# A mixer layer with product-key experts: scatters and first-stage gathers kept in the program's order on GpSimd, and a list's sort cut into four parts with a dense block between

## The chip, the cores and the metric

One core of a Trainium2 chip runs the whole kernel. The metric is the device time of one execution in microseconds; lower is better.

## The reference

One layer on 512 tokens of width 2048. A mixer (attention with forget gates beside a gated linear recurrence) comes first; its part of the kernel is not touched. Then comes the expert layer (PEER), where the change is:

```python
s1 = einsum(q[..., 0, :], k1); s2 = einsum(q[..., 1, :], k2)
v1, i1 = top_k(s1, 16); v2, i2 = top_k(s2, 16)
vs, ic = top_k(v1[..., :, None] + v2[..., None, :], 16)
e = i1[ic // 16] * 128 + i2[ic % 16]
w = softmax(vs)
act = gelu(einsum('thkd,td->thk', u[e], h)) * w
y = einsum('thk,thkd->td', act, vt[e])
```

Every token has 8 heads and picks 16 of 16384 experts in each. `u` and `vt` hold one row of 2048 floats for each expert. All arithmetic is in fp32; a matrix product is made of three products of a rounded and a remainder part.

## The kernel before

**Four token tiles of 128.** Three of them go through a dense first stage: for each of 128 blocks of 128 experts, `ublock` (L680) multiplies the block of `u` with the three tiles, applies gelu and stores the result in two tables in DRAM (`tab2`, `tab1`). The fourth tile is done row by row beside it, the *side work* (`side_work`, L748): 128 gathers of `u` rows, each followed by a product with the tokens on VectorE (L757), then 128 gathers of `v` rows, each added to a sum (L755). One gather brings one row for each of 128 tokens, 1 MB.

**A dense block** is two halves. Each half loads 512 KB of `u` on SyncE's queue (L98), rounds it on ScalarE (L93), takes the remainder on VectorE (L94), does 24 matmuls (L689) and ends with a call of `pump()`. A pump runs two things: 0.9 of a side gather (the gather on GpSimd, and the VectorE step for the gather two before), and one scatter, if any is queued. So 128 blocks carry 256 pumps and some 231 of the 258 side steps; the rest is sent out in the second stage, in equal shares over the first 68 chunks.

**Two lists** tell the second stage which experts any token of a tile uses. Making one has four steps.
- `halves_of` (L899): the weights of a tile are spread with one-hot products into `ws` (L906 to L913), 64 tokens at a time; each half ends with four stores of 1 MB into a table (L917) and four maxima (L918). Between the groups of four tokens it calls `ublocks`, at a pace set by `BH` or `BL`.
- `make_list` (L833): each of the 128 partitions sorts its 128 block numbers in descending order. A round is `V.max` (the eight largest, L821) and `V.match_replace` (strikes them out, L822); 16 rounds sort all. List 0, for two tiles, first sorts two short own lists of three rounds each.
- 16 or 20 columns that overflow are scattered by row to a list in DRAM: one indirect DMA on GpSimd for each column (L883, `one(i)`), queued in `scatters`, and at the end the read-back on SyncE's queue (L887).
- Between list 0 and list 1 the tokens of the third dense tile go through `topk` (L931 loads, L587 to L603) and `decode`.

**The second stage** goes through 171 chunks of 128 experts. `vchunk` gathers 128 `v` rows (1 MB) and their gelu values (`raw`), multiplies, splits and accumulates in PSUM (L988).

**What sets the order.** The source is traced from top to bottom; that is the program's order. When the program is built, each engine's and queue's instructions are put in one fixed order by simulating it: whenever an engine is free it gets, among the instructions whose inputs and buffers are ready by then, the one that stands first in the program. So what is ready early runs ahead of what is traced before it. `tc.keep_in_program_order(ins)` adds an order edge from the instruction that was traced just before `ins` on the same engine: `ins` is put behind it in that engine's order. It adds no semaphore wait. On the chip each engine follows its fixed order.

The calls of `ublocks` before: blocks 0 to 2 at the start, to 71 by the end of list 0's halves, then list 0's sort, to 75, `topk` to 81, list 1's halves to 116, list 1's sort, and to 128.

Of the kernel before, what the change touches and what calls it, by code (L numbers as in the profile page):

```python
# [27 lines left out]
LISTS = ((48, 16, 4), (66, 20, 5))  # L28
NONE = 24
B0 = 3  # L30
BH = 18
BL = 20
GRATE = 0.9
GLAG = 2
NAR = 5
# [23 lines left out]
def program(ctx: ExitStack, tc: tile.TileContext, a):  # L59
    nc = tc.nc  # L60
    V, A, PE, G = nc.vector, nc.scalar, nc.tensor, nc.gpsimd
# [45 lines left out]
    def rstd(pool, ss, n, scale):  # L107
        v = pool.tile([128, 16], F32, name="rs", tag="rs", bufs=4)[:, :n]
        A.activation(v, ss, AF.Sqrt, bias=eps, scale=scale)
        V.reciprocal(v, v)  # L110
        return v
# [23 lines left out]
    for half in range(2):  # L135
        r = raw.tile([128, 1024], F32, name="raw")[:1]
# [28 lines left out]
    def bank():  # L165
        return ps.tile([128, 512], F32, name="ps", tag="ps")
# [13 lines left out]
    with tc.tile_pool(name="pro", bufs=1, reuse_waits="tile") as pro:  # L180
# [7 lines left out]
        for t in range(NT):  # L188
# [7 lines left out]
            r = rstd(pro, ss, 1, 1.0 / D)  # L196
# [362 lines left out]
    with tc.tile_pool(name="wk2", bufs=12, reuse_waits="tile") as wk2:  # L559
        for q in range(4):  # L560
            pr = bank()
            for k4 in range(4):
                k = q * 4 + k4
# [81 lines left out]
    for h in range(H):  # L645
# [6 lines left out]
        for half in range(2):  # L652
            p = pbank()
            for hv in range(2):
                wh, wl = stream(a["w_q"][h * 2 + half, hv])
                for k8 in range(8):
                    k = hv * 8 + k8
# [7 lines left out]
            c0 = half * 128  # L665
# [16 lines left out]
    def ublock(b):  # L682
        p = pbank()
        for half in range(2):
            uh, ul = stream(a["peer_u"][b, half])
            for k8 in range(8):
                k = half * 8 + k8
                for i, (l, r) in enumerate(three(uh, ul, dh[k], dl[k])):
                    PE.matmul(p[:, :NDT], l[:, k8 * 128:k8 * 128 + 128], r, start=(k == 0 and i == 0),  # L689
                              stop=(k == KC - 1 and i == 2))  # L690
            pump()
        ge = gq.tile([128, NDT], F32, name="ge")
        A.activation(ge, p[:, :NDT], AF.Gelu_apprx_tanh)  # L693
        rows = slice(128 + b * 128, 256 + b * 128)
        nc.sync.dma_start(tab2[rows].rearrange("p (t x) -> p t x", t=2)[:, :, 0:128],
                          ge[:, 128:384].rearrange("p (t x) -> p t x", t=2))
        nc.sync.dma_start(tab1[rows, 0:128], ge[:, 0:128])
# [5 lines left out]
    blk = [0]  # L703
# [6 lines left out]
    def ublocks(upto):  # L710
        while blk[0] < upto:
            ublock(blk[0])
            blk[0] += 1
# [9 lines left out]
    ei = late.tile([128, H * 16], I32, name="ei")  # L723
# [16 lines left out]
    tabs = (tab2, tab1)  # L740

    def gather(out, src, idx):
        G.indirect_dma_start(out=out, out_offset=None, in_=src,  # L743
                             in_offset=bass.IndirectOffsetOnAxis(ap=idx, axis=0))

    NSIDE = 2 * H * 16 + GLAG

    def side_work():  # L748
        held = []
        n = H * 16  # L750

        def use():
            v, j, r = held.pop(0)
            if v:
                V.scalar_tensor_tensor(out=y0, in0=r, scalar=dots[:, j:j + 1], in1=y0, op0=OP.mult, op1=OP.add)  # L755
                return
            V.scalar_tensor_tensor(out=r, in0=r, scalar=1.0, in1=hrow, op0=OP.mult, op1=OP.mult,  # L757
                                   accum_out=dots[:, j:j + 1])
            if j == n - 1:
                A.activation(dots, dots, AF.Gelu_apprx_tanh)  # L760
                V.tensor_tensor(out=dots, in0=dots, in1=ew, op=OP.mult)

        for v in range(2):
            for j in range(n):
                r = gb.tile([128, D], F32, name="gr")
                gather(r, a["v_rows" if v else "u_rows"], ei[:, j:j + 1])
                held.append((v, j, r))
                if len(held) > GLAG:
                    use()
                yield  # L770
        while held:
            use()
            yield

    class Side:
        def __init__(self):
            self.it = side_work()
            self.n = 0
            self.due = 0.0
# [38 lines left out]
    def rounds(L, vals, n):  # L818
        for k in range(n):
            sl = slice(k * 8, k * 8 + 8)  # L820
            V.max(L[:, sl], vals[k % 2])  # L821
            V.match_replace(vals[1 - k % 2], L[:, sl], vals[k % 2], 0.0)  # L822
        return vals[n % 2]

    def rows_of(L, n, nm):
# [6 lines left out]
    def make_list(lt, Fs, n):  # L832
        c0, r, _ = LISTS[n]  # L833
        own = []
        cnt = lt.tile([128, 2], F32, name="lcnt")
        vals = [lt.tile([128, 128], F32, name=f"lv{i}") for i in range(2)]
        L = lt.tile([128, 128], F32, name="lf")
        fs = [lt.tile([128, 128], F32, name=f"lu{i}") for i in range(len(Fs))]
        for f, F in zip(fs, Fs):
            V.scalar_tensor_tensor(out=f, in0=F, scalar=0.0, in1=iota1, op0=OP.is_gt, op1=OP.mult)  # L840
        if len(Fs) == 1:
            V.tensor_copy(vals[0], fs[0])
        else:
            both = lt.tile([128, 128], F32, name="lboth")
            V.tensor_tensor(out=both, in0=fs[0], in1=fs[1], op=OP.min)
            for f in fs:
                V.tensor_tensor(out=f, in0=f, in1=both, op=OP.subtract)
            for i, f in enumerate(fs):
                rest = rounds(L, [f, vals[0]], NONE // 8)
                ig, iv = rows_of(L, NONE, f"own{i}")  # L850
                V.tensor_scalar(ig, ig, 2, i, op0=OP.mult, op1=OP.add)
                own.append((ig, iv))
                V.tensor_tensor(out=both, in0=both, in1=rest, op=OP.add)
            V.tensor_copy(vals[0], both)
        V.tensor_scalar(L, vals[0], 0.0, None, op0=OP.is_gt)
        V.tensor_reduce(cnt[:, 0:1], L, axis=AX.X, op=OP.add)
        rounds(L, vals, 16)
        ig, iv = rows_of(L, 128, n)
        V.tensor_scalar(cnt[:, 1:2], cnt[:, 0:1], float(-c0 - r), 0.0, op0=OP.add, op1=OP.max)
        V.tensor_scalar(cnt[:, 0:1], cnt[:, 0:1], float(-c0), 0.0, op0=OP.add, op1=OP.max)  # L860
        V.tensor_scalar(cnt[:, 0:1], cnt[:, 0:1], float(r), None, op0=OP.min)
        p = bank()
        PE.matmul(p[:, 0:1], tri, cnt[:, 0:1], start=True, stop=True)
        PE.matmul(p[:, 1:3], ones, cnt, start=True, stop=True)
        tot = lp1.tile([128, 3], F32, name=f"off{n}")
        V.tensor_copy(tot, p[:, 0:3])
        pos = lt.tile([128, 32], U32, name="lpos")[:, :r]
        V.tensor_scalar(pos, iota[:, :r], tot[:, 0:1], None, op0=OP.add)
        pc = lt.tile([128, 2, 32], U32, name="lpc")[:, :, :r]
        V.tensor_scalar(pc[:, 0], pos, 127, None, op0=OP.bitwise_and)  # L870
        V.tensor_scalar(pc[:, 1], pos, 7, None, op0=OP.logical_shift_right)
        pf = lt.tile([128, 2, 32], F32, name="lpf")[:, :, :r]
        V.tensor_copy(pf, pc)
        V.scalar_tensor_tensor(out=pf[:, 0], in0=pf[:, 0], scalar=float(r), in1=pf[:, 1], op0=OP.mult, op1=OP.add)
        V.tensor_scalar(pf[:, 1], iota[:, :r], cnt[:, 0:1], 65536.0, op0=OP.is_ge, op1=OP.mult)
        idx = lp1.tile([128, 32], I32, name=f"lidx{n}")[:, :r]
        V.tensor_tensor(out=idx, in0=pf[:, 0], in1=pf[:, 1], op=OP.add)
        views = dram_disjoint_views(lists[n], r)
        sg = lp1.tile([128, r], I32, name=f"sg{n}")
        sv = lp1.tile([128, r], I32, name=f"sv{n}")  # L880

        def one(i):
            G.indirect_dma_start(out=views[i], out_offset=bass.IndirectOffsetOnAxis(ap=idx[:, i:i + 1], axis=0),  # L883
                                 in_=ig[:, c0 + i:c0 + i + 1], in_offset=None, bounds_check=128 * r - 1, oob_is_err=False)

        def done():
            nc.sync.dma_start(sg, lists[n].rearrange("(p c) o -> p (c o)", p=128))  # L887
            V.tensor_scalar(sv, sg, -128, 0, op0=OP.add, op1=OP.max)

        scatters.extend([lambda i=i: one(i) for i in range(r)] + [done])  # L890
        return (ig, iv), (sg, sv), tot, own

# [30 lines left out]
    with tc.tile_pool(name="dz", bufs=1, reuse_waits="tile") as dz:  # L923
        Fs = [halves_of(dz, t, oT[t], tab2, t * 256 + 128, B0 + 2 * t * BH, BH) for t in range(2)]
        sets[0] = make_list(dz, Fs, 0)
    ublocks(B0 + 4 * BH)
    with tc.tile_pool(name="tp0", bufs=1, reuse_waits="tile") as tp0:
        tt0 = topk_tiles(tp0, 1)
        for h in range(H):
# [3 lines left out]
            if h % 2:  # L933
                ublocks(B0 + 4 * BH + h // 2 + 1)
        rows(decode(tp0, tt0))
        ublocks(B0 + 4 * BH + 6)
    with tc.tile_pool(name="dz2", bufs=1, reuse_waits="tile") as dz:
        sets[1] = make_list(dz, [halves_of(dz, 0, oT[2], tab1, 128, B0 + 4 * BH + 6, BL)], 1)
        ublocks(NB)
# [173 lines left out]
    r = inv(1)  # L1113
# [75 lines left out]
```

## Time and profile before

| | |
|---|---|
| median of 3 runs | 3143.48 us (3142.44 to 3146.86) |
| the profiled execution | 3144.75 us, of which the span is 3142.9 us |
| PE busy | 2872.5 us (91%) |
| VectorE (DVE) busy | 2487.0 us (79%) |
| ScalarE (ACT) busy | 1220.9 us (39%) |
| GpSimd (POOL) busy | 944.1 us (30%) |
| DMA | 869.31 MB, mean 277 GB/s |

All terms below are reckoned on the profiled execution; it is 1.27 us above the median. The dense stage lies between 1075 and 2380 us of the span, the second stage behind it. PEclk (the granted clock) is a share of TensorE's 2.4 GHz, DMA the mean busy share of 16 DMA engines.

### The profile page before, as it was taken

Reading aid. Unit: us, or ns where it says so; the run is one execution under the profiler, and the core shown is the slowest. Engines: PE = TensorE matmul, PEld = TensorE weight load, DVE = VectorE, ACT = ScalarE, POOL = GpSimd, SP = SyncE. Lnnn points to the kernel's source line nnn. Section 1 sums busy time; section 2 is a strip of 40 time slices with the busy share of each in tenths; the row PEclk is TensorE's granted clock in tenths of the full one; section 3 lists DMA queues with packets and bytes.
Section 4 is the critical chain, followed back from the end, with each engine's and each line's share of the span. In section 5 each row is a group of like instructions: output and inputs, shape, how many; then the busy total and the mean of one; then the engine's idle time right before and its main releaser. Section 6 shows DMA issues by size and latency. Waiting matters only on the chain.

```text
span 3142.9 us, 39160 instructions
## 1 busy us (share of the span) xinstructions
PE 2872.5 (91%) x14093; PEld 2501.5 (80%) x14093; DVE 2487.0 (79%) x4100; ACT 1220.9 (39%) x1653; POOL 944.1 (30%) x673
## 2 busy tenths in 40 slices
PE   7899999989999999988878999889998899988887
PEld 5677777778788899988868999879996688766665
DVE  6877777763368899999989998968888866677787
ACT  5322223662232333433322343413223455556665
POOL 0000000000020033222242322264447645567774
PEclk9999899999999999999988999989999999999998
DMA  9867777333322389999989999989999977779896
GB/s 343 291 222 235 239 236 238 106 107 128 114 90 94 117 297 379 340 306 295 294 270 357 351 347 352 314 319 404 404 403 386 386 278 272 260 270 344 320 327 228
DMA packets 329503, 869.31 MB, mean 277 GB/s; under 512 B 125682, under 2 KB 181362, under 8 KB 274388
## 3 DMA queue, kind: packets, MB, share of 16 engines
q0 software_dynamic: 72512, 477.03, 40.4%
q1 hardware_dynamic: 256352, 389.52, 36.8%
q8 instruction: 112, 1.84, 0.2%
q14 instruction: 91, 0.75, 0.1%
q10 hardware_dynamic: 436, 0.18, 0.0%
HBM read 805.38 MB, written 61.25 MB: 276 GB/s over the span
## 4 chain that ended last, share of the span: by engine, by line
PE 53%; DVE 17%; DMA 15%; issue 8%; ACT 3%; POOL 2%; SPq 1%; DVEq 0%; POOLq 0%; ACTq 0%
PE pj L689 25%; DMA araw<-w_ada 8%; PE ps L988 7%; PE pj L659 6%; DVE slo L94 5%; PE ps L525 4%; DVE gr L757 3%; PE pj L301 2%; PE ps L219 2%; DMA raw<-tab,ig 2%; DVE araw L147 2%; PE ps L912 2%; PE pj L988 1%; PE pj L525 1%; DMA tab<-ws 1%
## 5 line engine op out<-in xcount | busy, mean ns | idle before, releaser
L689 PE MATMUL pj<-dh,slo 128*128 128x384 f32 x2048 | 698.3, 343 | 59.4 <-DVE slo L94 57.9
L689 PE MATMUL pj<-dh,shi 128*128 128x384 f32 x2048 | 699.1, 341 | 29.0 <-ACT shi L93 26.4
L689 PE MATMUL pj<-dl,shi 128*128 128x384 f32 x2048 | 694.8, 339 | 1.3 <-issue 1.3
L93 ACT CAST shi<-raw 128x1024 fp32r<-128x1024 f32 (+1 forms) x402 | 418.3, 1048 | 634.1 <-PE pj L689 219.0
L94 DVE TENSOR_TENSOR slo<-raw,shi 128x1024 fp32r<-128x1024 f32 (+1 forms) x402 | 485.1, 1214 | 214.3 <-ACT shi L93 200.1
L689 PEld LDWEIGHTS pj<-dh,slo 128*128 128x128 f32 x2048 | 392.1, 192 | 70.6 <-DVE slo L94 68.7
L94 DVE TENSOR_TENSOR slo<-gr,shi 128x1024 fp32r<-128x1024 f32 x342 | 407.2, 1220 | 39.6 <-ACT shi L93 38.1
L689 PEld LDWEIGHTS pj<-dh,shi 128*128 128x128 f32 x2048 | 393.0, 192 | 30.9 <-ACT shi L93 27.9
L93 ACT CAST shi<-gr 128x1024 fp32r<-128x1024 f32 x342 | 345.0, 1046 | 157.0 <-PE ps L988 99.2
L743 POOL DMA_INDIRECT gr<-u_rows,ei x128 | 196.0, 1531 | 690.5 <-DVE gr L757 319.6
L689 PEld LDWEIGHTS pj<-dl,shi 128*128 128x128 f32 x2048 | 392.3, 192 | 2.1 <-issue 2.0
L988 PE MATMUL ps<-shi,gh 128*128 128x512 f32 x740 | 277.7, 418 | 64.3 <-ACT gh L93 36.7
L147 DVE SCALAR_TENSOR_TENSOR araw<-araw,sil 128x1024 f32<-128x1024 f32 x192 | 233.7, 1222 | 104.8 <-DMA araw<-w_ada 101.5
L755 DVE SCALAR_TENSOR_TENSOR y<-gr,dots,y 128x2048 f32<-128x2048 f32 x128 | 300.3, 2346 | 13.9 <-DMA gr<-v_rows,ei 12.6
L988 PE MATMUL ps<-slo,gh 128*128 128x512 f32 x740 | 298.0, 411 | 14.6 <-DVE slo L94 13.8
L743 POOL DMA_INDIRECT gr<-v_rows,ei x128 | 211.7, 1654 | 311.4 <-DVE y L755 204.6
L757 DVE SCALAR_TENSOR_TENSOR gr<-gr,hrow 128x2048 f32<-128x2048 f32 x128 | 291.5, 2279 | 11.3 <-DMA gr<-u_rows,ei 8.8
L988 PE MATMUL ps<-shi,gl 128*128 128x512 f32 x740 | 273.8, 401 | 2.1 <-DVE gl L94 2.1
L678 POOL CAST dh<-hh 128x384 fp32r<-128x384 f32 x16 | 10.3, 645 | 857.8 <-DVE hh L572 857.8
L693 ACT ACTIVATE ge<-pj 128x384 f32<-128x384 f32 x128 | 63.0, 492 | 459.0 <-PE pj L689 371.1
L988 PEld LDWEIGHTS ps<-shi,gh 128*128 128x128 f32 x740 | 145.5, 198 | 112.2 <-ACT gh L93 45.7
L301 PE MATMUL pj<-hh,shi 128*128 128x512 f32 x528 | 215.6, 408 | 3.9 <-ACT w L477 3.5
(353 smaller groups left out, 4966.7 us busy)
## 6 DMA issues: line engine op xcount, KB each, us to landing
raw<-peer_u SPq DMA_DIRECT2D x256, 512.0 KB
araw<-w_ada SPq DMA_DIRECT2D x192, 512.0 KB
raw<-w_in SPq DMA_DIRECT2D x66, 512.0 KB
tab<-ws SPq DMA_DIRECT2D x24, 1024.0 KB
raw<-w_out SPq DMA_DIRECT2D x32, 512.0 KB
raw<-w_q SPq DMA_DIRECT2D x32, 512.0 KB
tab<-ge SPq DMA_DIRECT2D x128, 128.0 KB
tab<-ge SPq DMA_DIRECT2D x128, 64.0 KB
```

What stands on the lines that cost most here:

```text
L93: A.copy(hi, src)
L94: V.tensor_tensor(out=lo, in0=src, in1=hi, op=OP.subtract)
L147: V.scalar_tensor_tensor(out=r, in0=r, scalar=1.0, in1=sil[:, half * 1024:half * 1024 + 1024], op0=OP.mult, op1=OP.mult, accum_out=acc[:, ...
L301: PE.matmul(p, l[:, k8 * 128:k8 * 128 + 128], r, start=(k == 0 and i == 0), stop=(k == KC - 1 and i == 2))
L525: PE.matmul(po[t], l[:, ts], r[:, sl], start=(k == 0 and i == 0), stop=(k == KC - 1 and i == 2))
L659: PE.matmul(p, l[:, k8 * 128:k8 * 128 + 128], r, start=(k == 0 and i == 0), stop=(k == KC - 1 and i == 2))
L689: PE.matmul(p[:, :NDT], l[:, k8 * 128:k8 * 128 + 128], r, start=(k == 0 and i == 0), stop=(k == KC - 1 and i == 2))
L693: A.activation(ge, p[:, :NDT], AF.Gelu_apprx_tanh)
L743: G.indirect_dma_start(out=out, out_offset=None, in_=src, in_offset=bass.IndirectOffsetOnAxis(ap=idx, axis=0))
L755: V.scalar_tensor_tensor(out=y0, in0=r, scalar=dots[:, j:j + 1], in1=y0, op0=OP.mult, op1=OP.add)
L757: V.scalar_tensor_tensor(out=r, in0=r, scalar=1.0, in1=hrow, op0=OP.mult, op1=OP.mult, accum_out=dots[:, j:j + 1])
L988: PE.matmul(banks[t][half * 2 + q2], l[:, ts], x[:, sl], start=first and i == 0, stop=end and i == 2)
```

## The change

```diff
-BH = 18
-BL = 20
+BH = 17
+BL = 17
+ROUNDS = 4
...
     def gather(out, src, idx):
-        G.indirect_dma_start(out=out, out_offset=None, in_=src,
-                             in_offset=bass.IndirectOffsetOnAxis(ap=idx, axis=0))
+        return G.indirect_dma_start(out=out, out_offset=None, in_=src,
+                                    in_offset=bass.IndirectOffsetOnAxis(ap=idx, axis=0))
...
-                gather(r, a["v_rows" if v else "u_rows"], ei[:, j:j + 1])
+                tc.keep_in_program_order(gather(r, a["v_rows" if v else "u_rows"], ei[:, j:j + 1]))
...
     def rounds(L, vals, n):
         for k in range(n):
             sl = slice(k * 8, k * 8 + 8)
-            V.max(L[:, sl], vals[k % 2])
+            tc.keep_in_program_order(V.max(L[:, sl], vals[k % 2]))
             V.match_replace(vals[1 - k % 2], L[:, sl], vals[k % 2], 0.0)
+            if k % ROUNDS == ROUNDS - 1 and k < n - 1:
+                ublocks(blk[0] + 1)
         return vals[n % 2]
...
-            G.indirect_dma_start(out=views[i], out_offset=bass.IndirectOffsetOnAxis(ap=idx[:, i:i + 1], axis=0),
-                                 in_=ig[:, c0 + i:c0 + i + 1], in_offset=None, bounds_check=128 * r - 1, oob_is_err=False)
+            tc.keep_in_program_order(G.indirect_dma_start(out=views[i], out_offset=bass.IndirectOffsetOnAxis(ap=idx[:, i:i + 1], axis=0),
+                                 in_=ig[:, c0 + i:c0 + i + 1], in_offset=None, bounds_check=128 * r - 1, oob_is_err=False))
```

All scatters, all 256 side gathers (also those sent in the second stage) and every `V.max` of a sort get an order edge. The gathers of `vchunk` get none. A sort of 16 rounds traces one dense block after rounds 4, 8 and 12. With the new `BH` and `BL` the calls of `ublocks` are: to 67 by the end of list 0's halves, 68 to 70 inside its sort, to 71, `topk` to 77, list 1's halves to 107, 108 to 110 inside its sort, and to 128.

## Rows read from the trace of the kernel before

**Rows 1.** All engines by stretch; columns: PE, PEld, DVE, ACT, POOL busy (count), PEclk, DMA, GB/s.
```profile
1590.00:1660.00 70.00, 48.89 (x258) 47.46 (x256) 58.45 (x186) 13.88 (x17) 32.51 (x25) 0.83 0.83 282
2045.00:2100.00 55.00, 42.42 (x217) 40.30 (x216) 32.27 (x75) 9.91 (x12) 34.15 (x26) 0.85 0.82 282
2100.00:2380.00 280.00, 276.34 (x1592) 275.07 (x1591) 234.36 (x138) 81.55 (x103) 129.69 (x73) 1.00 1.02 402
```

**Rows 2.** Stretches of the dense matmuls alone (L689): PE busy (count), PEld busy (count), clock.
```profile
1590.00:1660.00 70.00, 48.31 (x254) 46.94 (x252) 0.83 0.83 282
2045.00:2100.00 55.00, 42.08 (x213) 39.73 (x212) 0.85 0.82 282
2100.00:2380.00 280.00, 274.74 (x1580) 273.78 (x1579) 1.00 1.02 402
```

**Rows 3.** Timeline of POOL after list 0's sort: start, duration, instruction, idle before and releaser.
```profile
1602.34 0.94 POOL L743 DMA_INDIRECT gr<-u_rows,ei  x1 [12.54 <-DVE lv L822]
1610.99 2.82 POOL L883 DMA_INDIRECT list<-ig,lidx  x1 [7.71 <-DVE ig L828]
...
1617.60 3.04 POOL L883 DMA_INDIRECT list<-ig,lidx  x1 [0.30 <-issue]
...
1639.36 0.99 POOL L743 DMA_INDIRECT gr<-u_rows,ei  x1 [0.30 <-issue]
```

**Rows 4.** Timeline of DVE: first and last round of list 0's sort, and the next late product.
```profile
1595.74 0.29 DVE L821 MAX8 lf<-lv 128x8 f32<-128x128 f32 x1
...
1610.24 0.28 DVE L822 MATCH_REPLACE8 lv<-lf,lv 128x128 f32<-128x128 f32 x1
...
1645.06 2.29 DVE L757 SCALAR_TENSOR_TENSOR gr<-gr,hrow 128x2048 f32<-128x2048 f32 x1 [8.50 <-DMA gr<-u_rows,ei]
```

**Rows 5.** Timeline of PE: the first dense matmul after the sort of list 0.
```profile
1606.78 0.69 PE L689 MATMUL pj<-dh,shi 128*128 128x384 f32 x1 [9.25 <-ACT shi L93]
```

**Rows 6.** Timelines of POOL and DVE after list 1's sort.
```profile
2056.91 3.05 POOL L883 DMA_INDIRECT list<-ig,lidx  x1 [11.60 <-DVE iv L829]
...
2077.71 0.98 POOL L883 DMA_INDIRECT list<-ig,lidx  x1 [0.30 <-issue]
...
2088.72 0.99 POOL L743 DMA_INDIRECT gr<-v_rows,ei  x1 [0.30 <-issue]
...
2095.74 2.35 DVE L755 SCALAR_TENSOR_TENSOR y<-gr,dots,y 128x2048 f32<-128x2048 f32 x1 [10.76 <-DMA gr<-v_rows,ei]
```

**Rows 7.** Groups on POOL: 1100 to 2380 us (three rows), then 2380 to 2460 us.
```profile
L743 POOL DMA_INDIRECT gr<-u_rows,ei x128 | 196.0, 1531 | 690.5 <-DVE gr L757 319.6 <-PE pj L689 222.5 <-DVE o L911 67.4
L743 POOL DMA_INDIRECT gr<-v_rows,ei x112 | 184.5, 1647 | 306.5 <-DVE y L755 204.6 <-DVE o L911 75.2 <-issue 12.2
L883 POOL DMA_INDIRECT list<-ig,lidx x36 | 53.1, 1476 | 29.7 <-DVE iv L829 11.6 <-issue 10.4 <-DVE ig L828 7.7
...
L743 POOL DMA_INDIRECT gr<-v_rows,ei x16 | 27.2, 1698 | 4.9 <-issue 4.0 <-DVE slo L94 0.6 <-DVE gl L94 0.3
```

**Rows 8.** Second stage by stretch: matmuls L988 alone (first row), then all engines.
```profile
2380.00:2500.00 120.00, 92.76 (x359) 71.12 (x360) 0.90 0.99 394
...
2380.00:2500.00 120.00, 95.61 (x377) 73.68 (x377) 102.96 (x105) 44.75 (x62) 92.83 (x57) 0.90 0.99 394
2500.00:2740.00 240.00, 240.00 (x1030) 193.11 (x1029) 155.13 (x209) 124.73 (x158) 124.83 (x103) 1.00 0.78 277
```

**Rows 9.** POOL's gathers from 1126 to 1233 us (a group), its iota, DVE before it (timelines).
```profile
L743 POOL DMA_INDIRECT gr<-u_rows,ei x26 | 47.3, 1817 | 281.7 <-PE pj L689 222.5 <-DVE gr L757 40.7 <-DVE sm L635 4.1
...
1233.41 0.15 POOL L807 IOTA pm<- 128x1 f32 x1
...
1231.16 0.28 DVE L630 TENSOR_TENSOR se<-se,abf 128x128 f32<-128x128 f32 x1
```

**Rows 10.** All engines in the stretch between those gathers.
```profile
1126.00:1233.00 107.00, 102.71 (x582) 100.04 (x581) 104.45 (x96) 33.28 (x40) 46.86 (x26) 1.00 0.98 368
```

**Rows 11.** Timeline of SyncE's queue: the first loads of `topk`.
```profile
1611.61 1.73 SPq L931 DMA_DIRECT2D s<-sspill  x2
```

## The prediction

> **What bounds the kernel now.** I read the page first (PE is busy 91% of the span, but unevenly), then the stretches of the dense stage, then the timelines of POOL, VectorE and PE around the two places where the dense matmuls thin out. After 2100 us the stage runs as it should: clock 1.00, 1580 dense matmuls in 274.74 us of busy time [rows 2], 0.174 us each, so 8.35 us for a block of 48. VectorE is busy 234.36 of those 280 us [rows 1], so over 32.9 blocks it has 1.39 us of slack in each. Before that, two stretches fall far behind this pace. In 1590 to 1660 us, 254 matmuls are done [rows 2], worth 44.2 us, so 25.8 us are lost; in 2045 to 2100 us, 213, worth 37.1 us, so 17.9 us are lost. Together 43.7 us. The granted clock is 0.83 and 0.85 there: behind the idle gap of 9.25 us the first matmul takes 0.69 us [rows 5], so part of the time runs at the lower of the two levels (1.2 GHz). The loss by count includes that.
>
> What ends last in the two places is seen in two steps. First the sort: 16 rounds of list 0 stand in one lump on VectorE, from 1595.74 to 1610.52 us, 14.8 us with one product of 2.29 us inside [rows 4]. The remainders for the matmuls wait their turn behind it, and PE stands until 1606.78 [rows 5]. Then the scatters: 15 of list 0 follow one another on POOL from 1610.99 on, with 0.30 us between, and the next side gather starts only at 1639.36, 37 us after the one before [rows 3]. VectorE runs in order; it stands 8.50 us before the product of that late gather [rows 4], and the remainders behind the product stand with it. List 1 repeats this: scatters from 2056.91, the next gather at 2088.72, VectorE idle for 10.76 us before 2095.74 [rows 6], and busy in only 32.27 of 55 us [rows 1]. In the program, a scatter and a gather alternate; in the trace they don't, because all scatters of a list become ready together while the gathers wait for buffers.
>
> **The change part by part.**
>
> *Scatters and side gathers in program order.* No instruction is added; 36 scatters and 256 side gathers are placed. Between two scatters there is now about one gather (0.9 in a pump), so the run of 15 to 20 is broken up. POOL then has to do in half a block (4.17 us) one gather, 1.53 to 1.65 us in the mean, one scatter, 1.48 us, and two gaps of 0.30 us [rows 7, 3]: 3.6 to 3.7 us. That fits, so the gathers stay in step and I cost the scatters at nothing. The cover is 0.5 us a half. The bounds come from the longest scatter, 3.05 us, and the shortest, 0.98 us [rows 6]: with 3.05 us in all 36 halves POOL would need 1.65 + 3.05 + 0.60 = 5.3 us, 1.1 us over, 41 us in all; with 0.98 us, nothing. I stay near the mean, since it has both ends in it. VectorE's idle time before a late gather goes. The next thing to be late is a remainder behind a sort part.
>
> *The edge on the gathers reaches the iota.* The one iota of POOL is traced after the fourth side gather, and the trace has it at 1233.41 us, behind 26 gathers; it comes right after the last step of the third decode (1231.16) [rows 9], so I take it that its tile waits for that memory. From the fifth gather on, all gathers now queue behind the iota. At worst, 22 gathers wait until 1233, with 22 x 2.29 = 50 us of products. But VectorE is full there, 104.45 of 107 us [rows 10]. Without the products its other work is 54 us, so the decode and the iota come at about 1180 us and VectorE is never idle. The side work starts later and the list work sooner; I take 0, with 0 to 20 us as bounds (up to 20 if the products land where nothing else is left to overlap).
>
> *The sort in four parts.* Without its product the lump is some 12 us, 3 us a part. The parts after rounds 4, 8 and 12 are put behind the VectorE work of a dense block, including that block's product. What is queued behind a held `V.max` on VectorE is whatever was placed after it, remainders of later blocks above all, and PE waits for those. No semaphore wait is added. A part overruns the slack of its block by 3.0 - 1.39 = 1.6 us; three parts make 4.8 us a list. The first part stands in the open, 3 us a list, and the six rounds of list 0's own lists, 4.5 us, are not cut (three rounds reach no block). In all 9.6 + 6 + 4.5 = 20 us of the 43.7 stay. So the first stage gains 24 us. Bounds: all of the loss (44 us), and nothing.
>
> *BH, BL and the moved blocks.* The number of blocks is the same. Six stand inside sorts, and nine fewer inside the halves; each moves with two loads and two stores on SyncE's queue, past the table stores and the list read-backs there. The trace says that these numbers don't set the place anyway: at 2045 us, 1793 matmuls are left [rows 2], 37 blocks, where the program has list 1's sort 12 blocks before the end. The list work runs some 25 blocks ahead. I take 0, and as bounds nine blocks with or without their slack, 9 x 1.39 = 12.5 us either way.
>
> *Side gathers in the second stage.* The trace has 240 side gathers before 2380 us, 9 more than the program, and the other 16 in the next 80 us, 27.2 us plus 4.9 us of gaps on POOL [rows 7]. POOL and the DMA engines (0.99) are full there, and 359 matmuls are done in 120 us where 1030 take 240 [rows 8]: 84 us of work, 36 us lost. Now a side gather stands behind the table gather of its chunk: 0.4 a chunk. A chunk of 24 matmuls takes 5.6 us at full pace, so 80 us hold 14 chunks and 6 gathers, ten fewer, at 2.0 us each 20 us of POOL. Bounds are 0 and 20 us, as the stage's start costs something in any case; I take 10, between them, since the DMA engines bind beside POOL. The gathers that come later meet POOL busy in 125 of 240 us and DMA at 277 GB/s [rows 8]; twenty more megabytes make 360 GB/s, below the 394 to 402 that the full stretches move. They cost nothing, at most 5 us.
>
> **Sum.** 3144.75 - 24 - 10 = 3110.75 us on the profiled execution. The median is 1.27 us lower: 3109.5 us. The bounds with most weight (44 and 20 gained, or the parts that stay twice as dear) give this case 3083 to 3130 us.
>
> **The rivals.**
>
> *POOL is the limit while scatters run.* The scatters now stand beside a VectorE that is busy. The trace speaks for it: scatters took 2.82 and 3.04 us at the start of a run [rows 3] and 0.98 us where VectorE stood idle [rows 6]. With (2.82 + 3.04 + 0.98) / 3 = 2.28 us a scatter, a half needs 1.65 + 2.28 + 0.6 = 4.53 us, 0.36 us over 4.17, 13 us over 36 halves: 3122.5 us. Against it: the gathers themselves, at 1.53 to 1.65 us, already run beside a busy VectorE. The Trainium skill (SBUF — State Buffer, SBUF: two separate sides) says that VectorE and GpSimd share one pair of ports, that whichever starts first holds it for the whole instruction and that the other blocks; by this rule breaking up the run moves scatters from free to contended time. The trace agrees in direction, not in a proven cause.
>
> *The relief is not used.* The first loads of `topk` come at 1611.61 us [rows 11], 1 us after the sort. If their memory waits for the sort's end, `topk` and list 1 now start when block 70 is done, not at about 46 (71 - 25). In 24 blocks nothing but the first part of the sort fills VectorE's slack: 24 x 1.39 = 33 us, and the work comes back where VectorE is full. 3109.5 + 33 = 3142.5 us, no change. Against it: before, the slack after 2100 us was unused too, so that idle time may only change its place. That the edges leave the runs whole, because gathers were issued ahead, would also end near 3142; but an edge keeps gather and scatter alternating, so this is unlikely.
>
> *POOL blocked at a scatter (slower).* A scatter that isn't ready now blocks every side gather behind it. The place is the first pump of block 110, where the first scatter of list 1 stands. If the sort ends N blocks later than that, 1.8 N gathers are held, and are made up at 2.0 us each where POOL and DMA are full, at the start of the second stage. It decides from 17 gathers on, some ten blocks, where the gain of 34 us is gone; at 15 blocks, 27 gathers cost 54 us: 3109.5 + 54 = 3163.5 us. For it: with the delay above, list 1 loses its lead of 25 blocks. Against it: the lead is 25 blocks now, and VectorE without products does list work faster.
>
> **How the numbers follow.** About 0.2% (6.3 us) is what a measurement of this kernel can tell from no change. Chances: the forecast 0.60, POOL as the limit 0.15, relief not used 0.12, blocked POOL 0.13. The first two are faster, and a little of the third: 0.76. Same 0.11, slower 0.13. The range takes in the forecast's own 3083 to 3130 and the second and third cases, up to 3147, and leaves the blocked queue out.
>
> **What would show it.** Right: on POOL no run of scatters longer than two, VectorE's idle time before side products in those places near 0, at most 3 us of sort between two remainders, and the count of dense matmuls in 50 us after each list near 280. In the second stage, side gathers spread to about 2690 us. Wrong: a long wait of POOL before the first scatter of a list, VectorE idle in stretches where `topk` has not begun, or PE below full pace between 2500 and 2740 us.

## The result, and the profile after

The changed kernel takes 3116.05 us (median of 6 runs, 3113.47 to 3119.49); the kernel before, run beside it, 3142.96 us (6 runs, 3128.75 to 3146.86). The ratio is 0.9922, 95% interval 0.9902 to 0.9941: faster, by 0.8% or some 24.5 us. The forecast gain was 34 us; the time lies within the forecast's own range. The experiments show that the sum came out of partly wrong terms.

The profiled execution took 3117.84 us. I split each span in three: up to the first dense matmul, the dense stage (first start to last end of the dense matmuls), and the rest.

| | start | dense stage | rest | span |
|---|---|---|---|---|
| before | 1075.4 | 1306.7 | 760.8 | 3142.9 |
| after | 1072.6 | 1283.0 | 760.4 | 3116.0 |

The gain lies in the dense stage, 23.7 us; the second stage has none. First the stretches of the dense matmuls alone (L690 after) that answer to [rows 2]; columns as there:

```profile
1540.00:1580.00 40.00, 26.63 (x125) 25.49 (x124) 0.83 1.08 333
1580.00:1840.00 260.00, 260.00 (x1501) 259.70 (x1500) 1.00 0.99 383
1840.00:1880.00 40.00, 28.97 (x139) 28.33 (x138) 0.83 0.92 338
...
2260.00:2300.00 40.00, 24.19 (x119) 23.55 (x118) 0.79 0.76 294
```

From 1580 to 1840 us PE is never idle. Behind it, the two thin places are still there: 139 and 119 matmuls in 40 us, where 232 fit at full pace (1600 to 1640 us). POOL shows what stands there, in the timeline that answers to [rows 3] and [rows 6]:

```profile
1809.17 2.82 POOL L886 DMA_INDIRECT list<-ig,lidx  x1 [9.29 <-DVE ig L831]
1812.29 0.97 POOL L744 DMA_INDIRECT gr<-u_rows,ei  x1 [0.30 <-issue]
...
1819.97 1.01 POOL L886 DMA_INDIRECT list<-ig,lidx  x1 [0.30 <-issue]
...
1838.86 0.98 POOL L886 DMA_INDIRECT list<-ig,lidx  x1 [0.30 <-issue]
1840.15 0.99 POOL L744 DMA_INDIRECT gr<-v_rows,ei  x1 [0.30 <-DMA list<-ig,lidx]
```

Between 1819.97 and 1838.86 us stand ten scatters and no gather; list 1 has runs of nine and seven. The products behind the late gathers (timeline of DVE, for [rows 4]) wait as before, here and, with 9.62 us, in list 1's place (2269.05 us):

```profile
1846.21 2.35 DVE L756 SCALAR_TENSOR_TENSOR y<-gr,dots,y 128x2048 f32<-128x2048 f32 x1 [7.97 <-DMA gr<-v_rows,ei]
```

So the edge on the scatters did nothing. The instructions of the scatters' line say why; columns: engine, operation, count, shortest, median and longest ns, first and last start:

```profile
L886 POOLq MOVE  x36: 29/29/35, 1797.7 to 2265.3; - x36
L886 POOL DMA_INDIRECT list<-ig,lidx x36: 983/1007/3017, 1809.2 to 2273.8; - x36
```

Each scatter traces a register move first (its bounds check), so the instruction "traced just before it" on GpSimd is its own move, which need not wait for the list: the first one runs 11 us ahead of the first scatter. The program with the 36 scatter edges taken out has the same fixed order on all five engines. The edges on the gathers hold: a gather stays behind what was traced before it.

That is seen at the iota, which answers to [rows 9]:

```profile
1130.54 0.94 POOL L744 DMA_INDIRECT gr<-u_rows,ei  x1 [0.30 <-issue]
1180.34 0.13 POOL L808 IOTA pm<- 128x1 f32 x1 [48.86 <-DVE se L628]
1180.63 0.95 POOL L744 DMA_INDIRECT gr<-u_rows,ei  x1 [0.16 <-issue]
```

It stands at 1180 us, behind 4 gathers instead of 26, and the list work (the first one-hot matmul) begins at 1203.5 us where it began at 1259.2 us before. The side work that was not done there turns up in the second stage: 33 side gathers behind the last dense matmul, 16 before [rows 7].

```profile
L744 POOL DMA_INDIRECT gr<-v_rows,ei x33 | 47.7, 1447 | 10.1 <-issue 8.5 <-DVE gl L95 0.6 <-DVE slo L95 0.6
```

VectorE's sums over the dense stage agree (all engines: PE, PEld, DVE, ACT, POOL), first of the kernel before, then of the one after:

```profile
1075.00:2382.00 1307.00, 1203.62 (x6956) 1186.02 (x6955) 1183.96 (x1641) 422.09 (x501) 443.55 (x282) 0.96 0.94 337
```
```profile
1073.00:2356.00 1283.00, 1197.63 (x6945) 1186.42 (x6944) 1144.56 (x1620) 421.84 (x498) 390.43 (x266) 0.96 0.93 328
```

VectorE does 39.4 us less in the stage. The 17 gathers put off, at 2.3 us a product, make 39.1 of them.

The second stage, for [rows 8]:

```profile
2356.00:2476.00 120.00, 106.84 (x444) 83.96 (x443) 102.78 (x104) 52.12 (x68) 93.06 (x60) 0.94 0.98 388
2476.00:2716.00 240.00, 225.94 (x953) 178.48 (x952) 192.29 (x227) 116.03 (x156) 159.81 (x119) 0.99 0.94 358
```

These counts take in other matmuls as well. The second stage's own (L988 before, L991 after), in the 120 us from the last dense matmul on, first before, then after:

```profile
2382.10:2502.10 120.00, 94.86 (x367) 72.80 (x368) 0.90 1.00 398
```
```profile
2355.60:2475.60 120.00, 104.33 (x427) 82.33 (x428) 0.94 0.98 388
```

So the first 120 us hold 427 against 367, and the next 240 us 953 against 1030. At 0.233 us each (240 / 1030) that is 14.0 us won and 17.9 us lost.

One row was misread in the prediction. The idle 9.25 us of PE at 1606.78 [rows 5] I put down to the sort. ScalarE and SyncE's queue of the kernel before show another cause:

```profile
1605.68 1.04 ACT L93 CAST shi<-raw 128x1024 fp32r<-128x1024 f32 x1 [17.35 <-DMA raw<-peer_u]
...
1570.31 28.00 SPq L917 DMA_DIRECT2D tab<-ws  x3
1598.41 3.51 SPq L98 DMA_DIRECT2D raw<-peer_u  x1
```

The rounding waited 17.35 us for a load of `u`, and the load stood on SyncE's queue behind the four 1 MB table stores of a half, three of which (the row x3) took 28 us to issue. The cut sort changes nothing in that. The changed kernel has the same gap in the same place, though only four of the sort's 16 rounds stand there (1559 to 1562 us; the other twelve come, in parts, from 1783.70 to 1808.02 us, behind dense blocks that the program has far later):

```profile
1533.38 24.05 SPq L920 DMA_DIRECT2D tab<-ws  x3
1557.53 5.92 SPq L99 DMA_DIRECT2D raw<-peer_u  x1
...
1567.34 1.04 ACT L94 CAST shi<-raw 128x1024 fp32r<-128x1024 f32 x1 [14.14 <-DMA raw<-peer_u]
...
1568.43 0.69 PE L690 MATMUL pj<-dh,shi 128*128 128x384 f32 x1 [7.25 <-ACT shi L94]
```

This is the loss of 1540 to 1580 us in the first fence: 107 matmuls too few, 18.6 us at 0.174 us.

### The profile page after: what moved, and what is told of

It is laid out like the page before. It is cut to its first block, busy times and chain, and to the rows that moved or that the text cites. A ratio compares the mean times of both kernels' runs of the same rounds, so it can differ in the third digit from the quotient of the medians.

```text
span 3116.0 us, 39002 instructions
## 1 busy us (share of the span) xinstructions
PE 2859.3 (92%) x14093; PEld 2497.1 (80%) x14093; DVE 2487.7 (80%) x4100; ACT 1221.3 (39%) x1653; POOL 928.6 (30%) x673
## 4 chain that ended last, share of the span: by engine, by line
PE 56%; DVE 12%; DMA 10%; issue 7%; ACT 3%; POOL 2%; SPq 1%; another core or an unknown queue 0%; DVEq 0%; ACTq 0%; POOLq 0%
PE pj L690 25%; PE ps L991 11%; PE pj L660 6%; PE ps L526 4%; DMA araw<-w_ada 4%; DVE slo L95 4%; PE pj L302 3%; PE pj L991 2%; PE ps L915 2%; DVE gr L758 1%; DMA raw<-tab,igown 1%; PE pj L526 1%; DVE F L921 1%; ACT shi L94 1%; POOL gr L744 1%
## 5 line engine op out<-in xcount | busy, mean ns | idle before, releaser
L690 PE MATMUL pj<-dh,slo 128*128 128x384 f32 x2048 | 698.9, 343 | 53.7 <-DVE slo L95 53.5
L690 PE MATMUL pj<-dh,shi 128*128 128x384 f32 x2048 | 699.6, 342 | 21.1 <-ACT shi L94 21.1
L690 PE MATMUL pj<-dl,shi 128*128 128x384 f32 x2048 | 696.8, 340 | 0.0
L690 PEld LDWEIGHTS pj<-dh,slo 128*128 128x128 f32 x2048 | 392.4, 192 | 60.8 <-DVE slo L95 60.4
L690 PEld LDWEIGHTS pj<-dh,shi 128*128 128x128 f32 x2048 | 393.3, 192 | 22.2 <-ACT shi L94 22.2
L690 PEld LDWEIGHTS pj<-dl,shi 128*128 128x128 f32 x2048 | 392.5, 192 | 0.1
L744 POOL DMA_INDIRECT gr<-u_rows,ei x128 | 173.9, 1358 | 678.5 <-DVE gr L758 313.9
L991 PE MATMUL ps<-shi,gh 128*128 128x512 f32 x740 | 254.0, 414 | 73.3 <-ACT gh L94 42.0
L991 PE MATMUL ps<-slo,gh 128*128 128x512 f32 x740 | 297.4, 408 | 6.9 <-DVE slo L95 6.9
L744 POOL DMA_INDIRECT gr<-v_rows,ei x128 | 198.3, 1549 | 311.4 <-DVE y L756 161.3
L991 PE MATMUL ps<-shi,gl 128*128 128x512 f32 x740 | 275.2, 399 | 1.6 <-DVE gl L95 1.6
L991 PEld LDWEIGHTS ps<-shi,gh 128*128 128x128 f32 x740 | 143.9, 196 | 122.2 <-ACT gh L94 50.3
```

The lines of the kernel that those rows point to most:

```text
L744: return G.indirect_dma_start(out=out, out_offset=None, in_=src, in_offset=bass.IndirectOffsetOnAxis(ap=idx, axis=0))
L991: PE.matmul(banks[t][half * 2 + q2], l[:, ts], x[:, sl], start=first and i == 0, stop=end and i == 2)
```

## The experiments

Each ratio is to runs of the kernel before on the same chip, whose medians were 3138.89 to 3145.34 us. "Side" is the number of side gathers behind the last dense matmul; stages are of the one profiled execution, which lies within 7 us of the run's median but for e_nopool.

| run | edit | us | ratio, 95% interval | dense | rest | side |
|---|---|---|---|---|---|---|
| e_nopool | after, no edges on POOL | 3153.34 | 1.0045 [1.0025, 1.0065] | 1319.7 | 747.4 | 16 |
| e_nocut | after, sort whole | 3115.30 | 0.9912 [0.9887, 0.9937] | 1288.9 | 757.1 | 28 |
| e_side1 | after, second-stage gathers free | 3139.27 | 0.9992 [0.9979, 1.0006] | 1289.9 | 777.2 | 33 |
| e_alt | after, real alternation | 3102.05 | 0.9875 [0.9851, 0.9899] | 1273.3 | 749.2 | 30 |
| e_pm | after, iota early | 3130.54 | 0.9973 [0.9955, 0.9991] | 1303.1 | 753.0 | 25 |
| e_bh | before, BH = BL = 17 | 3141.39 | 1.0002 [0.9985, 1.0018] | 1310.4 | 753.8 | 16 |
| e_altnocut | e_alt, sort whole | 3098.41 | 0.9858 [0.9821, 0.9895] | 1277.2 | 748.7 | 25 |
| e_altq | e_alt, dense stores on ScalarE | 3114.72 | 0.9922 [0.9897, 0.9947] | 1280.5 | 758.3 | 30 |
| e_hold | before, four gathers behind the iota | 3145.48 | 0.9997 [0.9980, 1.0013] | 1287.1 | 786.8 | 28 |
| e_altpm | e_alt, iota early | 3128.84 | 0.9953 [0.9931, 0.9976] | 1309.1 | 751.3 | 24 |
| e_altrate | e_alt, more side work in blocks 46 to 70 | 3125.88 | 0.9943 [0.9923, 0.9962] | 1264.2 | 774.9 | 32 |
| e_two | before, hold and second-stage edges | 3116.64 | 0.9925 [0.9906, 0.9943] | 1293.3 | 742.7 | 28 |

The rest differs by some 7 us between e_bh and the kernel before, which have the same second stage: smaller differences of a part are not read.

**Which part of the change carries the gain?** Four runs undo or mend one part.

e_nopool:
```diff
-                tc.keep_in_program_order(gather(r, ...))
+                gather(r, ...)
-            tc.keep_in_program_order(G.indirect_dma_start(out=views[i], ...))
+            G.indirect_dma_start(out=views[i], ...)
```


> The changed kernel without the edges on scatters and side gathers; the cut sort and BH and BL stay. Theory (the cut sort and the later topk bring the gain of the dense stage; the edges on POOL bring little): 3108 to 3126 us, dense stage 1278 to 1292 us. Rival (the edges on the side gathers bring it): 3133 us or more, dense stage 1300 us or more.

3153.34 us: without the edges on POOL nothing is left of the gain. The cut sort and the moved blocks alone make the kernel slower by 0.45%. (The profiled execution of this run lies 14 us below its median, so its stages are not read.)

e_nocut:
```diff
-ROUNDS = 4
+ROUNDS = 99
```


> The changed kernel with the sorts in one lump (no dense block between, edges on V.max without effect); the edges on POOL and BH and BL stay. Theory (the cut brings the gain): 3130 to 3145 us, 14 to 22 us of dense matmuls lost in the lumps and the scatters early again. Rival (the edges on POOL bring the gain): 3110 to 3122 us.

3115.30 us, level with the changed kernel: the rival holds, the cut brings nothing that can be measured. List 1's whole sort (1987.5 to 2000.1 us there) lies in a gap that SyncE's queue makes anyway, with the table stores and then a dense block's store of 6.70 us:

```profile
1965.59 25.81 SPq L920 DMA_DIRECT2D tab<-ws  x3
...
1998.95 1.34 SPq L99 DMA_DIRECT2D raw<-peer_u  x3
...
2003.85 0.69 PE L690 MATMUL pj<-dh,shi 128*128 128x384 f32 x1 [7.11 <-ACT shi L94]
```

The next load goes out at 1998.95 us, when the sort is in its last two rounds.

e_side1:
```diff
-                tc.keep_in_program_order(gather(r, ...))
+                g = gather(r, ...)
+                if blk[0] < NB:
+                    tc.keep_in_program_order(g)
```


> The changed kernel with edges on the side gathers of the dense stage only; those sent in the second stage are free. Theory (spreading them over the second stage moves the loss and saves nothing): 3110 to 3122 us, second stage 756 to 766 us. Rival one (spreading them saved some 10 us that something else took back): 3124 us or more. Rival two (spreading them costs): 3108 us or less.

3139.27 us, rival one: 0.0070 (22 us) above the changed kernel by the ratios. With the same 33 side gathers free to crowd at its start, the rest takes 777.2 us, 16.8 us more than in the changed kernel. So the second stage's edges do pay, though the before/after split shows 0.4 us there: they offset what the 17 more gathers would cost.

e_alt:
```diff
+                lastg[0] = tc.keep_in_program_order(gather(r, ...))
...
-            tc.keep_in_program_order(G.indirect_dma_start(out=views[i], ...))
+            with tc.issue_after(lastg[0].ins):
+                G.indirect_dma_start(out=views[i], ...)
```


> The changed kernel, but each scatter is put behind the last side gather itself (the register move that comes with a scatter too), so that scatters and side gathers really alternate. Theory (the runs of scatters still cost PE some 16 and 20 us behind the two lists): 3085 to 3100 us, VectorE's longest idle time before a side product there below 4 us, dense stage 1245 to 1265 us long instead of 1283. Rival (what is lost there is VectorE's topk and list work, the runs cost nothing of their own): 3110 to 3122 us.

3102.05 us, 0.47% below the changed kernel by the ratios: a gain of some 14 us, where the theory had 16 to 31. The time lies outside both ranges, and the dense stage, 1273.3 us, outside the theory's. The long runs are gone (timeline of POOL):

```profile
1824.13 1.59 POOL L744 DMA_INDIRECT gr<-u_rows,ei  x1 [0.30 <-issue]
1826.03 1.01 POOL L889 DMA_INDIRECT list<-ig,lidx  x1 [0.30 <-issue]
1827.34 2.53 POOL L744 DMA_INDIRECT gr<-v_rows,ei  x1 [0.30 <-issue]
1830.17 1.72 POOL L889 DMA_INDIRECT list<-ig,lidx  x1 [0.30 <-issue]
```

VectorE's longest idle time before a side product is now 1.43 us in list 0's place and 1.27 us in list 1's, below the 4 us of the theory. But most of the gain does not lie where the runs stood. From 2220 to 2340 us there are 586 dense matmuls in e_alt and 578 in the changed kernel; from 1820 to 1980 us, 791 against 779. Between the two, where list 1's one-hot products and table stores stand and hardly any scatter, e_alt (first) is 58 ahead, 10.1 us at 0.174 us:

```profile
1980.00:2220.00 240.00, 211.26 (x1115) 192.96 (x1114) 0.98 0.98 337
```
```profile
1980.00:2220.00 240.00, 201.91 (x1057) 183.93 (x1056) 0.95 0.96 324
```

The stage as a whole is 9.7 us shorter. Why that stretch runs better was not isolated. So the edit is worth some 14 us, but it is not shown that the broken runs are. In list 0's place VectorE is the next limit, busy in 20.00 of 20 us in six of the seven slices from 1840 to 1980 us. In list 1's place PE waits for roundings on ScalarE (7.7 of the 10.5 us that it waits in 2220 to 2345 us), whose loads go out four at a time behind the stores of two blocks.

**A rhythm of the loads?** e_altq:
```diff
-        nc.sync.dma_start(tab2[rows]..., ge[:, 128:384]...)
-        nc.sync.dma_start(tab1[rows, 0:128], ge[:, 0:128])
+        nc.scalar.dma_start(tab2[rows]..., ge[:, 128:384]...)
+        nc.scalar.dma_start(tab1[rows, 0:128], ge[:, 0:128])
```


> The kernel in which scatters and side gathers alternate, with the two stores of each dense block issued from ScalarE's queue and no longer from SyncE's. After list 1's scatters have begun (2220 us to the end of the dense stage) that kernel has lost 4 us in four of six stretches of 20 us: PE waits for the rounding on ScalarE, the loads go out four at a time behind the stores of two blocks, and the granted clock is 0.91. Theory: a load that stands behind a store on SyncE's queue waits for the gelu of a block that is not yet done; with the stores on ScalarE, right behind the gelu, the loads go out one by one and the 15 to 19 us of that stretch are gone: 3083 to 3090 us. Rival one: the rhythm comes from the order on ScalarE itself (four roundings between two gelus) and stays: 3097 to 3107 us. Rival two: the stores' issue on ScalarE delays roundings everywhere and the time rises to 3110 us or more.

The place is mended; dense matmuls there, e_alt first, then e_altq:

```profile
2220.00:2340.00 120.00, 109.73 (x586) 106.84 (x585) 0.94 0.95 352
```
```profile
2220.00:2340.00 120.00, 114.94 (x654) 112.68 (x653) 1.00 1.00 383
```

68 more matmuls, 11.8 us at 0.174 us, and the clock is at 1.00. The total is not: 3114.72 us, rival two by the number, though its reason is not shown. The dense stage is 7.2 us longer than e_alt's and the rest 9.1 us, both near the size that is not read. What the other places lost I did not isolate.

**The other terms, one at a time.** e_bh:
```diff
-BH = 18
-BL = 20
+BH = 17
+BL = 17
```


> The kernel before with BH = BL = 17 and nothing else. Theory (the step of the prediction): the moved blocks do not set where the list work stands, so they are worth nothing: 3137 to 3149 us. Rival one, they are worth nine blocks' slack: 3130 us or less, or 3155 us or more. Rival two: any shift of blocks makes a new fixed order on all engines, which moves the time by 10 us or so either way without a cause in the numbers themselves; then it is outside 3137 to 3149 us as well, and the loss by stretches differs in places that have no block moved.

Ratio 1.0002 [0.9985, 1.0018]: the moved blocks are worth nothing, as forecast.

e_altnocut (e_alt with `ROUNDS = 99`):

> The kernel in which scatters and side gathers do alternate, with the sort of 16 rounds left whole (no dense block inside). Theory: the cut sort is worth little on this order as well, since the remainders are up to two blocks ahead when a sort begins: 3097 to 3108 us, no gap of PE over 3 us at a sort. Rival, the prediction's step: with the scatters out of the way, the whole sort stands alone and shows as two gaps on PE of 9 us and the lower clock behind them: 3114 us or more.

3098.41 us, the theory's number, and the fastest kernel of the study (beside e_alt's 3102.05 their intervals overlap). The whole sort costs nothing on this order either. PE does show a gap of 9.52 us at list 1's sort (1976.5 to 1988.7 us), against the theory's "no gap over 3 us". It is again the loads': the queue is held by four table stores and a block's store of 8.42 us behind them.

```profile
1955.05 22.74 SPq L923 DMA_DIRECT2D tab<-ws  x4
...
1987.06 1.15 SPq L99 DMA_DIRECT2D raw<-peer_u  x2
```

e_pm:
```diff
+    pm = const.tile([128, 1], F32, name="pm")
+    G.iota(pm, pattern=[[0, 1]], base=0, channel_multiplier=1, ...)
...
-    pm = lp1.tile([128, 1], F32, name="pm")
-    G.iota(pm, pattern=[[0, 1]], base=0, channel_multiplier=1, ...)
```


> The changed kernel with one thing moved: the iota that makes pm is traced at the start of the program, beside the other constant, so that from the fifth side gather on nothing is queued behind it; the edges and the cut sort stay. Theory: the hold of the gathers at the iota is a gain (in the changed kernel the list work starts at about 1200 us, 50 us earlier than before, because VectorE has no side products to do in the third decode). Without it the gathers run from 1126 us on, the list work starts at about 1250 us again, and the dense stage is 10 to 15 us longer: 3126 to 3132 us. Rival, the step of the prediction (the hold costs or brings nothing, because the side work that starts later has to be made up): 3111 to 3121 us, the dense stage within 5 us of 1283.

3130.54 us, as the theory had it; the dense stage is 20 us longer (1303.1 against 1283.0), where the theory had 10 to 15. The one-hot matmuls, first of the changed kernel, then of e_pm, up to 1300 us:

```profile
L915 PE MATMUL ps<-o,o x126: 271/275/275, 1203.5 to 1298.0; 128*128 128x128 f32 x126
```
```profile
L915 PE MATMUL ps<-o,o x83: 270/275/275, 1256.4 to 1300.0; 128*128 128x128 f32 x83
```

The start falls back to 1256.4 us, nearly that of before. Of the 23.7 us of dense stage, 20 hang on one iota. e_altpm asks whether that and the alternation are one gain:

> The kernel in which scatters and side gathers alternate, with the iota traced at the start, so without the hold. Theory: the hold (about 20 us of dense stage) and the alternation (some 14 us) are separate gains: 3114 to 3124 us, the list work starting at about 1250 us. Rival: they are two ways to the same gain, and with true alternation the late start of the list work costs little: 3098 to 3109 us.

3128.84 us: not one gain, and above the theory's range too. With alternation the hold is worth 0.0078 (24 us), without it 0.0051 (16 us). What alternation is worth without the hold (0.9953 beside 0.9973) the overlapping intervals leave open.

**The hold alone, and a price for it.** e_hold:
```diff
-                gather(r, ...)
+                g = gather(r, ...)
+                if not v and 4 <= j < 8:
+                    tc.keep_in_program_order(g)
```


> The kernel before with four order edges and nothing else: side gathers 4 to 7 of u are put behind what GpSimd was given just before them, which is the iota (its place moves from behind 26 gathers to behind 4). No scatter, no other gather and no sort is touched. Theory: the hold behind the iota alone carries the gain of the dense stage, about 20 us as in the run without it: dense stage 1281 to 1292 us, time 3118 to 3128 us. Rival one: the hold pays only together with the edges on the later gathers (the list work starts earlier but gives the time back at the runs of scatters): dense stage 1297 us or more, 3134 us or more.

Half of each. The dense stage is 1287.1 us, 19.6 shorter with four order edges, as the theory said. The total is 3145.48 us, ratio 0.9997, as rival one had it, though not for its reason: the time is lost again in the second stage, where the rest grows from 760.8 to 786.8 us. All engines in its first 360 us:

```profile
2357.00:2477.00 120.00, 96.10 (x379) 74.09 (x378) 106.39 (x98) 43.00 (x55) 99.20 (x59) 0.90 0.99 391
2477.00:2717.00 240.00, 221.88 (x921) 176.47 (x921) 162.86 (x206) 114.96 (x150) 139.90 (x104) 0.96 0.84 305
```

28 free side gathers crowd it, 12 more than before. The last run adds what this lacks. e_two:
```diff
-                if not v and 4 <= j < 8:
+                if not v and 4 <= j < 8 or blk[0] == NB:
```


> The kernel before with two of the change's effects and nothing else: the four order edges that hold the side gathers behind the iota, and an edge on each side gather that is traced in the second stage. No edge on a scatter, on the other side gathers of the dense stage, or in a sort; the sort whole; BH and BL as before. Theory: these two carry the whole gain, since the hold shortens the dense stage by 20 us by leaving some 12 side gathers more to the second stage, and the edges there let them cost nothing: dense stage 1282 to 1292 us as with the hold alone, the rest 750 to 762 us (786.8 with the hold alone), time 3108 to 3122 us. Rival: the broken runs of scatters or the cut sort are part of the gain, or the spread needs the edges ahead of it: 3128 us or more.

3116.64 us, ratio 0.9925 [0.9906, 0.9943], the same as the whole change's 0.9922. The same stretches:

```profile
2372.00:2492.00 120.00, 106.07 (x449) 84.51 (x448) 97.33 (x101) 52.95 (x66) 79.20 (x58) 0.96 0.92 353
2492.00:2732.00 240.00, 228.32 (x960) 179.99 (x959) 190.80 (x227) 116.88 (x157) 159.62 (x119) 0.99 0.94 358
```

449 and 960 matmuls where the hold alone had 379 and 921: 109 more, 25 us, with the same 28 side gathers; their mean on POOL falls from 1615 to 1247 ns. Two effects carry the whole change: side work is held back early in the dense stage, and what is left over is spread over the second. The time is the theory's, its split is not quite: the dense stage, 1293.3 us, is a little above the theory's range and the rest, 742.7 us, below. The hold does not pay without the spread (e_hold and e_side1 are both at no change). The spread without the hold keeps about a third of the gain (e_pm, 0.9973, which has the other edges and the cut sort as well); the spread alone, on the kernel before, was not run.

e_altrate tried to move the left-over into VectorE's slack at 1580 to 1780 us:
```diff
-    todo.append(lambda: side.send(GRATE))
+    todo.append(lambda: side.send(1.2 if 46 <= blk[0] < 71 else GRATE))
```


> The kernel in which scatters and side gathers alternate, with 1.2 in place of 0.9 side gathers a pump in blocks 46 to 70, which run at about 1580 to 1780 us, where VectorE is busy 15.4 to 17 of 20 us and PE loses nothing. Theory: fifteen side gathers come out of the second stage (15 left there, 30 now) and cost nothing where they go, since a pump has some 0.7 us of VectorE free in the mean and needs 0.3 x 2.3 us: dense stage within 4 us of 1273, the rest 5 to 10 us shorter: 3091 to 3098 us. Rival: VectorE or GpSimd is over its limit there and the dense stage pays: 3101 us or more.

3125.88 us, slower than e_alt, as the rival's number had it, but not its way: the dense stage is 9 us shorter than e_alt's, and the rest 25.7 us longer. POOL runs 49 instructions in that stretch, one more than in e_alt, and 32 side gathers still come late. The rate only traces them earlier. So most now stand ahead of the second stage's chunks in the program instead of between them, and its start is crowded: 352 matmuls in 120 us.

```profile
2343.00:2463.00 120.00, 89.56 (x352) 68.91 (x351) 94.36 (x87) 38.94 (x51) 100.19 (x66) 0.86 0.97 380
```

## Why the prediction was right, and where its reasons were wrong

The time lies in the range: 3109.5 us forecast, 3116.05 measured. That is partly luck. Of the 34 us forecast, the dense stage's 24 came from a cause that the text priced at nothing, and the second stage's 10 did not come. Term by term:

- **"The run of 15 to 20 is broken up": wrong.** The step took the diff at its word. The edge ties a scatter to its own register move, and the text discarded the rival that the runs stay whole for a wrong reason ("an edge keeps gather and scatter alternating"). Runs of nine and ten stayed (15 and 18 before), and so did DVE's idle 7.97 us. Real alternation (e_alt) is worth 14 us more, some 10 of them in a stretch without scatters. The longest scatter before was 3.10 us, not 3.05, which moves a bound by 2 us.
- **"The sort in four parts": wrong about what stood there.** PE's gap at the sort is the loads' wait behind table stores on SyncE's queue; I stopped at the releaser on ScalarE and did not follow it to ScalarE's own wait. The cut is worth nothing (e_nocut, e_altnocut), and without the edges the kernel that has it is 0.45% slower than before (e_nopool).
- **"First stage gains 24 us": right in size by luck, from another cause.** It gained 23.7; 20 of them hang on the hold at the iota (e_pm; 19.6 with the hold alone, e_hold), which I priced at 0 with 0 to 20 us as a cost. Its place, 1180 us, was right; "VectorE is never idle" was not quite, as it is busy in 49.91 of the 54 us from 1126 us on. The missing step: 17 products of 2.3 us leave a stage in which VectorE is near its limit, and the list work starts 56 us earlier. Number and place of the gathers cannot be told apart fully: with 25 left over, the stage took 1277.2 us (e_altnocut) and 1303.1 (e_pm).
- **BH, BL at 0: right** (e_bh).
- **Second stage, 10 us: wrong, it came out at 0.4.** The start won 14.0 us, but the end did not cost "at most 5". The gathers that come later cost 17.9 us, with 33 left and not 25; POOL is then busy in 160 and not 125 of 240 us, and PE in 226 of 240, one of the text's own signs of being wrong. Against free gathers of the same number the edges are worth some 22 us by the ratios (e_side1 beside the changed kernel, e_two beside e_hold).
- **The rivals.** "POOL is the limit" was not put to the test by the change, as nothing alternated; in e_alt, scatters do become dearer, 1.67 us in the mean beside 1.54 in the changed kernel (1.87 and 1.01 in the median), but not the 2.28 us of the rival, and POOL is busy in at most 16.67 of 20 us in list 1's place. "The relief is not used" had its premise right and its price wrong: `topk` now begins at 1808.51 us (timeline of SyncE's queue, for [rows 11]),

```profile
1808.51 1.24 SPq L934 DMA_DIRECT2D s<-sspill  x2
```

where the sort ends, some 246 us behind the sort's first part. Nothing is lost up to there (1501 matmuls in 260 us), and with the whole sort and an early `topk` (e_nocut) the total is level: the slack only changes its place, as the text said against this rival. The queue blocked at a scatter did not come: the scatters start as soon as a list is ready, with 9.29 and 12.24 us of idle time on POOL ahead of the first (7.71 and 11.60 before [rows 3, 6]).

Not tried: taking the 1 MB table stores off SyncE's queue, ahead of the loads. It bears on the places at 1540 to 1580 us (18.6 us) and 2160 to 2200 us (155 dense matmuls where 232 fit, 13.4 us; four such stores again, 16.75 us). How much of that it would give back is open.

## What to carry to other kernels

Check in the built order that an order edge reaches what it is meant for: an instruction that sets a register first is tied to that, and an edge on its neighbours may do the whole work. Follow an idle engine's releaser one step further, to what that engine itself waited for, before a lump that stands beside the gap is blamed. Work that is put off is not gone: look where it lands, and spread it there, for putting it off may be worth nothing without that.

## What the runs showed that I had not expected

Three 1 MB stores held SyncE's queue for 24 to 28 us at the end of list 0's halves (24.05 in the changed kernel, at a DMA share of 1.08), and with it the loads behind them; ScalarE stood 14.14 us and PE 7.25 us for that. The four stores of the other halves of these two kernels took 12 to 20 us. The same side gather cost GpSimd 1615 ns in the mean where 28 of them crowd the start of the second stage, and 1247 ns where they are spread.
